# A finer cut around the end of each filter unit, and a denser schedule of weight preparation, beside attention

## The chip, the cores and the metric

The kernel runs on 1 core of a Trainium2 chip. The metric is the device time of one execution in microseconds (us); less is better. Inputs and outputs are in float32.

## The reference

Two layers act on 2048 tokens of width 1024. The first has a pooling mixer beside attention (6 query heads, 2 key heads, 2304 keys: 256 of the context and 2048 of the tokens). The second has a long convolution (Hyena) beside a Fourier mixer. The change touches the stage that computes attention and, beside it, the filters of the second layer's convolution and its prepared weights. Cut to that:

```python
s = einsum('bqhgd,bkhd->bhgqk', q, k) * scale     # attention, layer 0
p = softmax(s, axis=-1)
yb = einsum('bhgqk,bkhd->bqhgd', p, v) * silu(b_gate)
...
h = (hdn @ w3).reshape(L, 2, 2, 768)              # filters, layer 1
h = h * decay
h = h / (sum(abs(h), axis=(0, 2)) + EPS)          # one sum for each filter
kf = fft(concat(h[:, :, 0], 0, reversed h[:, :, 1]))
```

## The kernel before, in words

The stages run one after the other: projections of layer 0 (to about 605 us), attention (to about 1776 us), the output projection of layer 0 with the first columns of layer 1, then layer 1. In the attention stage the order of every engine's instructions is the order in which the Python code records them; nothing is moved there by a planner. Names used below: PE multiplies, DVE, ACT and POOL are vector engines, SP issues the DMAs. Each engine takes its instructions in the order given.

**Attention.** There are 96 blocks of 128 queries; two blocks, one even and one odd, make a pair of 256 queries of one head, so there are 48 pairs, here numbered 0 to 47. A string in `BLOCK` (L44) lists what a block records, token by token: `S0` to `S4` are the scores of the *next* block against 512 keys (three matmuls each, L315 to L317, then a maximum on DVE, L1323), `M` the maximum over all, `E0` to `E4` the exponentials on ACT (L1334), `Z` their sum, `T0` to `T4` the transposition of this block's exponentials on PE (L1345) with a split into a high and a low part (ACT L309, DVE L312), `V0` to `V4` the products with the values (L1357 to L1361). `D` and `N` finish the pair before: ACT puts the reciprocal sums on a diagonal, PE multiplies that by ones (`prb`, L1374), and DVE multiplies the result with the gate and the output (`rb`, L1376 and L1377). After each even block SP stores `rb` and loads the queries of two pairs later.

**Filters.** `F` takes one step of the generator `filters` (L1119); `f` does so only in every `MORE`-th pair. There are 12 units (6 channel groups by 2 orders). A unit has 8 groups of two steps: one with the product `hacc` (L1194), which DVE multiplies with the decay into `ht` (L1195) and reduces into `rd` (L1198), and one with the product `fa` (L1231), which ACT copies into `fX` (L1232). Both products share one PSUM buffer, `psF`, so each of them waits until the one ahead has been read. In the last group come two steps more: DVE sums `rd` over the 8 groups into `rs` (L1204), PE multiplies `rs` by ones (`smacc`, L1207), and DVE makes the scales and `sd` from it (`scaled`, from L1213); the last `fa` (L1229) needs `sd`. That makes 18 steps for a unit. Then the unit's transform of length 16 is queued for POOL (L155, L158, L193), in pieces that `some` (L1131) hands out at nearly every later step, up to 4.4 us of planned POOL time each; a transform takes 13 such pieces. The spectrum `fX` is stored four pieces later.

**Weight preparation.** `p` takes one step of the generator `weights` (L1399). First come 23 pieces of the second layer's input weights: SP loads `wraw`, one step on ACT copies it into the high part of `wodd` (L1409), one step on POOL subtracts to get the low part (L1411), two steps on SP stores it and, in the same step, loads the next piece. `wraw` has two buffers and `wodd` one. Then come 32 pieces of the two output weights, with one more stage: POOL multiplies `wraw` by a gate (L1431) one step after the load, and two steps after that ACT copies. A piece of the first kind takes 4 steps, one of the second 6. At the end come two small products `fnp` on PE (L1446). All in all that is 92 + 192 + 12 steps. With six `p` in a pair they would take over 49 pairs; when the filters are through, `fill` (L1469) runs what is left of `weights` at once, then frees the memory, and from then on the blocks follow the third and fourth string and each `F` takes two steps of `wout` (L1386), which loads the 8 output weights `w` of layer 0 and the first two pieces of `y`.

**After attention** the output projection starts with `oacc` (L315 to L317); it needs `w` and the split `y` (ACT L1628, DVE L1629).

Of the kernel before, what the change touches and what calls it, by code (L numbers as in the profile page):

```python
# [20 lines left out]
P = 128  # L21
# [20 lines left out]
PAIRS = [(n, N2 - n) for n in range(1, 8)] + [(0, 8)]  # L42

BLOCK = [  # L44
# [204 lines left out]
def tile_net(ctx, tc, i, k, out, keep=None):  # L249
# [230 lines left out]
            split_to(hf[:, :w], hi[:, :w], lo[:, :w], v, lo_eng[m % 2])  # L480
            yield 1.3, 0.0

    LASTE, LASTR, GATE2, FOLD1, HALF, SUM0, SUM1, ADDF, FEW, LASTW, IN_C, FFT_US, FFT_LATE, FILTER_X, HL, DR, DE, EW0, EW1, SPLIT, SUMMED, QSEL, CV0, CV1, CV2, CV3, COL, NW0, NW1, FIRST_Z, MORE, X0_SQ, X0_STEP, TRAIL, C_EARLY, A_TURN, A_SLOW, A_AHEAD, A_W, A_PACE, LAG0, FOLD, WAIT, AHEAD, LAG, APART, LOW, W_LOAD, W_HIGH, W_LOW, ADDED, SLOW = 0, 0.5, 5, 6, 1.5, 0.2, 1.5, 3, 9, 3.5, 25, 4.4, 4, 2, 3, 4, 4, 8.0, 2.5, 15, 0.5, 1, 14, 12, 8, 15, 5, 24, 0, 20.0, 8, [7, 7, 11, 11], (0, 0, 0, 0, 2, 2, 2, 2), 11, 1, 2.5, 0.25, 3.5, 4, 1.05, 7, 2, 6.0, 2.5, 5, 5, 2, 6, 6, 4, 8, 1.02

    xr = i["x"][0].rearrange("(p b) d -> p b d", b=N2)
    outr = out[0].rearrange("(p b) d -> p b d", b=N2)
# [632 lines left out]
    def filters(st, psum, tag, after):  # L1119
# [59 lines left out]
        for u in range(2 * NCH):  # L1179
            j, o = u // 2, u % 2  # L1180
            w3, skr = got.pop(u)
            rd = sp.tile([P, 8, P], F32, tag="rd", name="rd")
            X = sp.tile([P, 2, N2, P], F32, tag="X", name="fX", bufs=FILTER_X)
            for grp, (n, m) in enumerate(PAIRS):
                last = grp == 7
                if (u, grp) != (2 * NCH - 1, 7):
                    fetch(u + grp // 7, (grp + 1) % 8)
                dec, hd = got.pop((u, grp))
                ht = sp.tile([P, 2, 2, P], F32, tag="ht", name="ht", bufs=2)
                acc = psum.tile([P, 2, 2, P], F32, tag=tag, name="hacc")  # L1190
                for q in range(2):
                    for x in range(2):
                        w = w3[:, x, ::-1] if q else w3[:, x]
                        pe.matmul(acc[:, q], hd[:, q, :], w, start=x == 0, stop=x == 1)  # L1194
                after(1, lambda: v.tensor_mul(ht, acc, dec.unsqueeze(2).to_broadcast([P, 2, 2, P])))  # L1195
                yield
                some()
                v.tensor_reduce(out=rd[:, grp, :], in_=ht.rearrange("p a d b -> p b (a d)"), axis=AX.X, op=ALU.add,  # L1198
                                apply_absolute_value=True)
                if u + 1 < 2 * NCH and grp in (3, 6):  # L1200
                    (fetch_w3 if grp == 3 else split_w3)(u + 1)
                if last:
                    rs = sp.tile([P, P], F32, tag="rs", name="rs")
                    v.tensor_reduce(out=rs, in_=rd.rearrange("p a b -> p b a"), axis=AX.X, op=ALU.add)  # L1204
                    yield
                    sm = psum.tile([P, 512], F32, tag=tag, name="smacc")
                    pe.matmul(sm[:, 0:1], rs, ones[:, 0:1], start=True, stop=True)  # L1207
                    pe.matmul(sm[0:1, P : 2 * P], ones[:, 0:1], rs, start=True, stop=True)
                    sd = sp.tile([P, 2, 2, P], F32, tag="ht", name="sd", bufs=2)

                    def scaled():
                        idx = o * NCH + j
                        v.tensor_scalar(out=sc_n[:, idx : idx + 1], in0=sm[:, 0:1], scalar1=EPS, scalar2=None, op0=ALU.add)  # L1213
                        rw = sp.tile([1, P], F32, tag="rw", name="rw")
                        v.scalar_tensor_tensor(out=rw, in0=sm[0:1, P : 2 * P], scalar=EPS, in1=skr, op0=ALU.add, op1=ALU.mult)
                        v.reciprocal(sc_n[:, idx : idx + 1], sc_n[:, idx : idx + 1])
                        v.tensor_add(ht[0:1, 0, 0, :], ht[0:1, 0, 0, :], rw)
                        v.memset(ht[0:1, 0, 1, :], 0.0)
                        v.tensor_add(sd[:, 0], ht[:, :, 0], ht[:, :, 1])
                        v.tensor_sub(sd[:, 1], ht[:, :, 0], ht[:, :, 1])  # L1220


                    after(2, scaled)
                    yield
                fa = psum.tile([P, 2, 2, P], F32, tag=tag, name="fa")
                for r in range(2):
                    for q, b in enumerate((n, m)):
                        if last:
                            pe.matmul(fa[:, r, q], dft[:, b, r, :], sd[:, r, q], start=True, stop=True)  # L1229
                        else:  # L1230
                            pe.matmul(fa[:, r], dft[:, b, r, :], ht[:, q], start=q == 0, stop=q == 1)  # L1231
                after(3, lambda: s.copy(X[:, :, n : m + 1 : m - n, :], fa))  # L1232
                yield
                if last:
                    T = sp.tile([P, 2, N2, P], F32, tag="T", name="fT")
                    ops += [(0.04 + 2.05 * us, fn) for fn, us in fft16(g, X, T, False, g, True)]
                    ops.append((0.0, (specd[j][o], X)))
                some()
# [20 lines left out]
    with ExitStack() as st:  # L1259
# [108 lines left out]
        def finish(key):  # L1368
            h, tb = key
            gr = groups.pop(key)  # L1370
            tl = slice(tb * 256, (tb + 1) * 256)
            pr = psT.tile([P, 2, P], F32, tag="pt", name="prb")
            for b, dg in enumerate(dgs.pop(key)):
                pe.matmul(pr[:, b, :], ones, dg, start=True, stop=True)  # L1374
            rb = sp.tile([P, 256], F32, tag="rb", name="rb")
            v.tensor_mul(rb, pr.rearrange("p a b -> p (a b)"), gr["sg"])  # L1376
            v.tensor_mul(rb, gr["o"], rb)  # L1377
            stores.append((y0d[2 + h][:, tl], rb))

        def store():  # L1380
            while stores:
# [17 lines left out]
        def weights():  # L1399
# [22 lines left out]
            for n, (src, dst) in enumerate(((i["ev_w_out"][0], wevd), (i["od_w_out"][0], wod))):  # L1422
                for half in range(2):
                    hl = slice(half * 512, half * 512 + 512)
                    gb = wp.tile([P, 512], F32, tag="gate", name="wgb")
                    sy.dma_start(gb, gated[n].rearrange("(o a) b -> o (a b)", o=1)[:, hl].to_broadcast([P, 512]))
                    for kk in range(KD):
                        raw = raws()
                        sy.dma_start(raw, src[kk * P : (kk + 1) * P, hl])
                        yield  # L1430
                        g.tensor_mul(raw, raw, gb)  # L1431
                        yield
                        yield
                        yield from parts(raw, dst[kk][:, :, hl])
            fw = raws().rearrange("p (a e) -> p a e", a=2)
# [49 lines left out]
        with tc.manual_schedule(engines=EVERY):  # L1485
# [53 lines left out]
            values(before, 4)  # L1539
            diagonals(before)  # L1540
            finish(before)
            store()
            while queue:
                fill()
# [875 lines left out]
```

## Time and profile before

| | us |
|---|---|
| median of 3 runs | 3170.09 |
| lowest and highest | 3164.2, 3178.07 |
| the profiled execution's own time | 3180.38 |
| its span, first to last instruction | 3178.6 |
| PE busy, of the span | 2935.4 |
| DVE, ACT, POOL busy | 2146.7, 1325.2, 1131.8 |
| granted TensorE clock, mean | 0.968 |

PE is busy 92% of the span, the others 36% to 68%. A busy PE is not a PE at its peak, since matmuls are pipelined and their ends are modelled. In the rows of a timeline the first number is the start, the second the duration, and brackets hold the idle time ahead and what ended it. In rows of waits the numbers are the total in us, the count and the longest.

### The profile page before, as it was taken

What the parts mean: (1) busy time and instruction counts of PE and PEld (TensorE: products, weight loads), DVE (VectorE), ACT (ScalarE), POOL (GpSimd) and SP (SyncE); (2) the same over time, 40 slices, a digit from 0 to 9 for tenths busy, and PEclk for the clock granted to TensorE, in tenths of its full rate; (3) what the DMA queues carried; (4) which work ended last, traced back from release to release, by engine and by line L of the source; (5) the groups of instructions that cost most, each with busy time, mean ns of one, the idle gap of its engine ahead of it and who ended that gap; (6) DMA issues with size and microseconds to landing.
All of it is one profiled execution on the core that took longest, in us unless ns stands there. A gap on an engine that the chain in (4) does not pass through costs nothing. (4 is left out here: it accounts for less than half of the span.)

```text
span 3178.6 us, 46875 instructions
## 1 busy us (share of the span) xinstructions
PE 2935.4 (92%) x16969; PEld 2519.8 (79%) x16969; DVE 2146.7 (68%) x3981; ACT 1325.2 (42%) x3047; POOL 1131.8 (36%) x1091
## 2 busy tenths in 40 slices
PE   7899999799999999999986999999989999988799
PEld 4898888688888888888875778777878787874577
DVE  4676436477777777777764343377789797978556
ACT  4444545365555555555554232322323222232223
POOL 3122222127768787777772344001010000101110
PEclk9999999899999999999998999999999999999899
DMA  6466335533433334333325676688898989876875
GB/s 219 149 203 206 119 134 165 177 98 123 128 124 120 110 121 131 112 107 113 114 77 193 213 265 244 241 267 275 267 310 272 292 280 307 274 251 184 217 206 175
DMA packets 346707, 602.74 MB, mean 190 GB/s; under 512 B 41894, under 2 KB 216168, under 8 KB 336490
## 3 DMA queue, kind: packets, MB, share of 16 engines
q1 hardware_dynamic: 321322, 516.63, 47.8%
q0 software_dynamic: 25152, 83.10, 11.2%
q8 instruction: 134, 2.20, 0.3%
q14 instruction: 99, 0.81, 0.1%
HBM read 376.80 MB, written 187.18 MB: 177 GB/s over the span
## 5 line engine op out<-in xcount | busy, mean ns | idle before, releaser
L312 DVE TENSOR_TENSOR pl<-pt,ph 128x512 fp32r<-128x512 f32 (+1 forms) x480 | 300.1, 634 | 160.0 <-ACT ph L309 153.6
L155 DVE TENSOR_TENSOR gB<-gB 128x256 f32<-128x256 f32 (+3 forms) x442 | 351.6, 845 | 51.5 <-ACT gB L1927 47.7
L1334 ACT ACTIVATE pb<-S,mx 128x512 f32<-128x512 f32 (+1 forms) x480 | 310.7, 658 | 177.5 <-DVE mx L1326 143.3
L315 PE MATMUL dacc<-dh,dw 128*128 128x512 f32 x768 | 311.4, 405 | 46.5 <-DMA dh<-h1T 45.4
L309 ACT CAST ph<-pt 128x512 fp32r<-128x512 f32 (+1 forms) x480 | 256.2, 557 | 216.9 <-PE pt L1345 215.0
L316 PE MATMUL dacc<-dh,dw 128*128 128x512 f32 x768 | 304.4, 396 | 0.0
L317 PE MATMUL dacc<-dh,dw 128*128 128x512 f32 x768 | 304.1, 396 | 0.0
L1323 DVE TENSOR_REDUCE mx<-S 128x1 f32<-128x512 f32 (+1 forms) x480 | 279.5, 629 | 8.9 <-PE S L317 8.7
L1345 PE MATMUL pt<-ident,pb 128*128 128x128 f32 x1728 | 251.3, 275 | 21.4 <-ACT pb L1334 20.0
L312 POOL TENSOR_TENSOR wl<-raw,wh 128x256 fp32r<-128x256 f32 x160 | 134.8, 873 | 373.3 <-ACT wh L309 347.6
L1357 PE MATMUL o<-ph,vh 128*128 128x256 f32 x864 | 237.9, 306 | 0.2
L1345 PEld LDWEIGHTS pt<-ident,pb 128*128 128x128 f32 x1728 | 200.2, 141 | 41.3 <-ACT pb L1334 29.8
L315 PE MATMUL S<-kh,qh 128*128 128x512 f32 (+1 forms) x480 | 200.0, 417 | 30.1 <-DVE pl L312 15.4
L1358 PE MATMUL o<-ph,vl 128*128 128x256 f32 x864 | 220.4, 286 | 1.8 <-DMA vl<-vl 1.8
L155 POOL TENSOR_TENSOR fX<-fT 128x256 f32<-128x256 f32 (+2 forms) x168 | 219.2, 1328 | 2.6
L315 PEld LDWEIGHTS dacc<-dh,dw 128*128 128x128 f32 x768 | 147.7, 192 | 85.0 <-DMA dh<-h1T 43.4
L155 POOL TENSOR_TENSOR fT<-fX 128x1024 f32<-128x1024 f32 (+2 forms) x120 | 190.8, 1622 | 58.4 <-ACT fX L1232 56.6
L315 PE MATMUL acc<-wh,hh 128*128 128x256 f32 x672 | 198.8, 296 | 5.4 <-DVE hh L311 2.6
L317 PE MATMUL acc<-wh,hl 128*128 128x256 f32 x672 | 194.0, 289 | 1.0 <-DVE hl L312 0.9
L316 PE MATMUL acc<-wl,hh 128*128 128x256 f32 x672 | 194.1, 289 | 0.9 <-POOL wl L312 0.8
L316 PE MATMUL S<-kl,qh 128*128 128x512 f32 (+1 forms) x480 | 182.2, 379 | 1.3 <-DMA kl<-kT1l 1.3
L317 PE MATMUL S<-kh,ql 128*128 128x512 f32 (+1 forms) x480 | 181.9, 379 | 0.0
(475 smaller groups left out, 7397.5 us busy)
## 6 DMA issues: line engine op xcount, KB each, us to landing
dh<-h1T SPq DMA_DIRECT2D x172, 512.0 KB
spec<-fX SPq DMA_DIRECT2D x12, 2048.0 KB
dw<-wi SPq DMA_DIRECT2D x48, 512.0 KB
gK<-spec SPq DMA_DIRECT2D x48, 512.0 KB
raw<-in_ev_w_in_dram SPq DMA_DIRECT2D x160, 128.0 KB
u<-dev SPq DMA_DIRECT2D x70, 256.0 KB
cu<-u POOLq DMA_DIRECT2D x17, 1024.0 KB, 8.3
wmb<-in_w_mod_dram SPq DMA_DIRECT2D x16, 1024.0 KB
```

Source lines behind the costliest of these rows:

```text
L155: put(out, lambda: v.tensor_tensor(out=out, in0=in0, in1=in1, op=op))
L309: s.copy(hi, src)
L312: lo_eng.tensor_sub(lo, src, hi.bitcast(F32))
L315: pe.matmul(acc, ah, bh, start=first, stop=False)
L316: pe.matmul(acc, ah, bl, start=False, stop=False)
L317: pe.matmul(acc, al, bh, start=False, stop=last)
L1323: v.tensor_reduce(out=B["mx"][:, c : c + 1], in_=S[:, :n], axis=AX.X, op=ALU.max)
L1334: s.activation(B["pb"][:, c * 512 : c * 512 + n], B["S"][c][:, :n], AF.Exp, bias=B["mx"][:, 5:6], accum_out=B["sm"][:, c : c + 1])
L1345: pe.transpose(pt[:, t, :], B["pb"][:, (4 * c + t) * P : (4 * c + t + 1) * P], ident)
L1357: pe.matmul(gr["o"], vh[:, a, :], ph[:, t, :], start=a == 0, stop=False)
L1358: pe.matmul(gr["o"], vl[:, a, :], ph[:, t, :], start=False, stop=False)
```

## The change

It has five edits, all in the attention stage.

1. `MORE` goes from 8 to 2: the `f` step is taken in every second pair instead of every eighth.
2. A unit of filters takes 20 steps instead of 18. The sum over the groups is made in two parts: groups 0 to 3 go into `rd[:, 4]` in group 5, and the five columns 4 to 8 into `rs` at the end, two tokens after their step begins. A step stands between that and the product `smacc`, and another between `scaled` and the last `fa`; both hand out a piece of the transform.
3. The even block's string gets one `p` more, so there are seven in a pair.
4. In the 32 pieces with a gate, ACT's copy stands one step behind POOL's product instead of two: a piece takes 5 steps, and the whole of `weights` 92 + 160 + 12.
5. The two products of `rb` are recorded two tokens after `N`, and flushed at the end of the stage.

```diff
-    "T0 p S0 S1 F S2 S3 S4 M T1 f p F D V3 V4 E1 N E3 T2 E0 T3 p E4 E2 F T4 Z",
+    "T0 p S0 S1 F S2 S3 S4 M T1 f p F D V3 V4 E1 N E3 T2 E0 T3 p E4 E2 F T4 p Z",
...
-            rd = sp.tile([P, 8, P], F32, tag="rd", name="rd")
+            rd = sp.tile([P, 9, P], F32, tag="rd", name="rd")
...
-                v.tensor_reduce(out=rd[:, grp, :], in_=ht.rearrange("p a d b -> p b (a d)"), axis=AX.X, op=ALU.add,
+                v.tensor_reduce(out=rd[:, grp + grp // 4, :], in_=ht.rearrange("p a d b -> p b (a d)"), axis=AX.X, op=ALU.add,
                                 apply_absolute_value=True)
...
+                if grp == 5:
+                    v.tensor_reduce(out=rd[:, 4, :], in_=rd[:, :4].rearrange("p a b -> p b a"), axis=AX.X, op=ALU.add)
                 if last:
-                    rs = sp.tile([P, P], F32, tag="rs", name="rs")
-                    v.tensor_reduce(out=rs, in_=rd.rearrange("p a b -> p b a"), axis=AX.X, op=ALU.add)
+                    rs = rd[:, 0, :]
+                    after(2, lambda: v.tensor_reduce(out=rs, in_=rd[:, 4:].rearrange("p a b -> p b a"), axis=AX.X, op=ALU.add))
+                    yield
+                    some()
                     yield
...
                     after(2, scaled)
+                    yield
+                    some()
                     yield
...
-            v.tensor_mul(rb, pr.rearrange("p a b -> p (a b)"), gr["sg"])
-            v.tensor_mul(rb, gr["o"], rb)
-            stores.append((y0d[2 + h][:, tl], rb))
+
+            def gated():
+                v.tensor_mul(rb, pr.rearrange("p a b -> p (a b)"), gr["sg"])
+                v.tensor_mul(rb, gr["o"], rb)
+                stores.append((y0d[2 + h][:, tl], rb))
+
+            after(2, gated)
...
                         g.tensor_mul(raw, raw, gb)
-                        yield
                         yield
                         yield from parts(raw, dst[kk][:, :, hl])
...
             finish(before)
+            flush()
             store()
```

Edit 1 is the one number `MORE` in the long line of numbers at L483.

Three places show what moves. The first is PE in the even block of pair 3 or so, at the `f` token. Before, the product `hacc` is followed by the values:

```order
L1345 MATMUL pt<-ident,pb 128x128 x4
L1194 MATMUL hacc<-w3s,hd 128x256 x4
L1357 MATMUL o<-ph,vh_6890 128x256
L1358 MATMUL o<-ph,vl_6891 128x256
L1357 MATMUL o<-ph,vh_6890 128x256
```

Now `fa` of the same group stands right behind it:

```order
L1351 MATMUL pt<-ident,pb 128x128 x4
L1194 MATMUL hacc<-w3s,hd 128x256 x4
L1237 MATMUL fa<-ht,fdft 128x256 x4
L1363 MATMUL o<-ph,vh_6890 128x256
L1364 MATMUL o<-ph,vl_6891 128x256
```

The `f` of a pair has moved a product of the filters to where another one follows at once. It does so in every second pair now.

The second place is POOL late in a transform, beside the pieces with a gate (`wraw<-wraw,wgb` is the product with the gate, `wodd<-wraw,wodd` the subtraction that follows ACT's copy). Before:

```order
L158 TENSOR_SCALAR fX<-fX 128x4x128
L1431 TENSOR_TENSOR wraw<-wraw,wgb 128x512
L158 TENSOR_SCALAR fT<-fT 128x4x128
L155 TENSOR_TENSOR fX<-fX,fT 128x4x128
L155 TENSOR_TENSOR fX<-fT,fX 128x4x128
L155 TENSOR_TENSOR fX<-fT 128x2x2x128 x2
L1411 TENSOR_TENSOR wodd<-wraw,wodd 128x512
L1431 TENSOR_TENSOR wraw<-wraw,wgb 128x512
```

Now, in a transform of the same phase:

```order
L155 TENSOR_TENSOR fT<-fX,fT 128x4x128
L155 TENSOR_TENSOR fT<-fT,fX 128x4x128
L155 TENSOR_TENSOR fX<-fT 128x4x128
L155 TENSOR_TENSOR fT<-fT 128x4x128
L1441 TENSOR_TENSOR wraw<-wraw,wgb 128x512
L1421 TENSOR_TENSOR wodd<-wraw,wodd 128x512
L155 TENSOR_TENSOR fX<-fT 128x2x128 x4
```

Five instructions of the transform stood between the product and the subtraction; now none does, and more of them stand ahead of the product.

The third place is SP at the end of the stage (`w0_n` are the output weights of layer 0, `cxt` the residual rows, `y0_n<-y0_85` the pieces of `y`, `y0_85<-rb` the stores of finished pairs). Before:

```order
L261 DMA w0_6_20296<-we6_215 128x2048
L261 DMA w0_7_20298<-we7_216 128x2048
L1246 DMA y0_20395<-y0_85 128x8x128
L1246 DMA y0_20397<-y0_85 128x8x128
L261 DMA y0_85<-rb_20411 128x256
L1618 DMA cxt_20579<-in_x_dram 128x2048
L1618 DMA cxt_20581<-in_x_dram 128x2048
```

Now:

```order
L1628 DMA cxt_20579<-in_x_dram 128x2048
L1628 DMA cxt_20581<-in_x_dram 128x2048
L261 DMA y0_85<-rb_20527 128x256
L261 DMA w0_6_20531<-we6_215 128x2048
L261 DMA w0_7_20533<-we7_216 128x2048
L1252 DMA y0_20538<-y0_85 128x8x128
L1252 DMA y0_20540<-y0_85 128x8x128
```

The last two weights and the first pieces of `y` have moved behind the residual rows and behind the store of the last pair.

More of the change, by code (lines that the diff above doesn't have):

```diff
@@ L481, in modulated_steps @@
             yield 1.3, 0.0
-    LASTE, LASTR, GATE2, FOLD1, HALF, SUM0, SUM1, ADDF, FEW, LASTW, IN_C, FFT_US, FFT_LATE, FILTER_X, HL, DR, DE, EW0, EW1, SPLIT, SUMMED, QSEL, CV0, CV1, CV2, CV3, COL, NW0, NW1, FIRST_Z, MORE, X0_SQ, X0_STEP, TRAIL, C_EARLY, A_TURN, A_SLOW, A_AHEAD, A_W, A_PACE, LAG0, FOLD, WAIT, AHEAD, LAG, APART, LOW, W_LOAD, W_HIGH, W_LOW, ADDED, SLOW = 0, 0.5, 5, 6, 1.5, 0.2, 1.5, 3, 9, 3.5, 25, 4.4, 4, 2, 3, 4, 4, 8.0, 2.5, 15, 0.5, 1, 14, 12, 8, 15, 5, 24, 0, 20.0, 8, [7, 7, 11, 11], (0, 0, 0, 0, 2, 2, 2, 2), 11, 1, 2.5, 0.25, 3.5, 4, 1.05, 7, 2, 6.0, 2.5, 5, 5, 2, 6, 6, 4, 8, 1.02
+    LASTE, LASTR, GATE2, FOLD1, HALF, SUM0, SUM1, ADDF, FEW, LASTW, IN_C, FFT_US, FFT_LATE, FILTER_X, HL, DR, DE, EW0, EW1, SPLIT, SUMMED, QSEL, CV0, CV1, CV2, CV3, COL, NW0, NW1, FIRST_Z, MORE, X0_SQ, X0_STEP, TRAIL, C_EARLY, A_TURN, A_SLOW, A_AHEAD, A_W, A_PACE, LAG0, FOLD, WAIT, AHEAD, LAG, APART, LOW, W_LOAD, W_HIGH, W_LOW, ADDED, SLOW = 0, 0.5, 5, 6, 1.5, 0.2, 1.5, 3, 9, 3.5, 25, 4.4, 4, 2, 3, 4, 4, 8.0, 2.5, 15, 0.5, 1, 14, 12, 8, 15, 5, 24, 0, 20.0, 2, [7, 7, 11, 11], (0, 0, 0, 0, 2, 2, 2, 2), 11, 1, 2.5, 0.25, 3.5, 4, 1.05, 7, 2, 6.0, 2.5, 5, 5, 2, 6, 6, 4, 8, 1.02
     xr = i["x"][0].rearrange("(p b) d -> p b d", b=N2)
```

## The prediction

> **What bounds the kernel now.** I read the page first, then busy time by stretches of the attention stage, then the waits of that stage, then single rows.
>
> The page gives each engine's share, and the span in 40 slices:
>
> ```profile
> PE 2935.4 (92%) x16969; PEld 2519.8 (79%) x16969; DVE 2146.7 (68%) x3981; ACT 1325.2 (42%) x3047; POOL 1131.8 (36%) x1091
> POOL 3122222127768787777772344001010000101110
> ```
>
> PE sets the time. POOL, at 36% overall, is 70% to 80% busy in slices 10 to 20, which is the stage that the change edits. By stretches (columns: from:to, length, then each engine's busy time, granted clock, DMA share, GB/s) that is a generic pair, a pair with a unit's end, a pair with its `f`, the last pairs one by one, and 60 us over one whole transform:
>
> ```profile
> 731.60:754.50 22.90, 22.62 (x151) 20.59 (x150) 16.96 (x33) 13.93 (x36) 22.37 (x25) 1.00 0.33 97
> 754.50:779.10 24.60, 22.59 (x159) 20.22 (x159) 19.77 (x35) 13.82 (x36) 9.18 (x8) 1.00 0.48 168
> 800.90:826.90 26.00, 24.19 (x162) 22.03 (x161) 18.25 (x34) 14.12 (x36) 25.30 (x25) 1.00 0.34 102
> 1634.20:1655.90 21.70, 18.54 (x126) 16.00 (x125) 13.16 (x29) 12.45 (x33) 21.23 (x22) 1.00 0.21 61
> 1655.90:1682.40 26.50, 21.08 (x126) 18.26 (x125) 13.43 (x29) 12.34 (x33) 25.13 (x24) 0.87 0.22 77
> 1682.40:1730.50 48.10, 25.31 (x135) 20.82 (x134) 13.76 (x30) 15.21 (x38) 6.34 (x5) 0.75 0.48 174
> 1730.50:1749.20 18.70, 17.62 (x127) 15.80 (x126) 13.19 (x29) 12.06 (x32) 0.00 (x0) 1.00 0.73 283
> 783.80:843.80 60.00, 57.91 (x388) 53.01 (x387) 43.77 (x84) 34.92 (x92) 58.90 (x50) 1.00 0.34 102
> ```
>
> A generic pair is full on PE (22.62 of 22.90). Two kinds of place are not: pairs with a unit's end (2 us idle), and the three stretches from 1634, where the filters' products have run out and weight preparation has not. There a pair needs no more than the 18.70 of the row at 1730.50, and takes up to 48.10. In the 60 us over a transform POOL is busy for 58.90: it has no slack. The waits of the stage (engine, line, what released it: total, times, longest):
>
> ```profile
> PE S L315 <- DVE pl L312: 11.9, 6, 4.6
> ...
> PE fa L1229 <- DVE sd L1219: 7.8, 4, 2.8
> ACT wodd L1409 <- POOL wraw L1431: 7.3, 2, 4.9
> PE smacc L1207 <- DVE rs L1204: 6.3, 6, 1.9
> ```
>
> The second and fourth row are PE's waits at a unit's end; ACT waits for POOL's gate product only twice so far.
>
> **The change, part by part.**
>
> *Drain gone: -36.* Weight preparation has 92 + 192 + 12 steps at six a pair, 49 pairs, and so is unfinished at pair 45. The three stretches from 1634.20 take 21.70 + 26.50 + 48.10 = 96.3 us; three pairs at 18.70 are 56.1; 40.2 are lost. Now 264 steps at seven a pair end in pair 38, inside attention. The two products `fnp` do not vanish; warm they cost PE about 2.0 each, as the eight matmuls `fa` of the same shape here (cold, after 16.81 idle, they took 3.75):
>
> ```profile
> 814.05 1.99 PE L1231 MATMUL fa<-ht,fdft 128*128 128x256 f32 x8 [1.58 <-DVE ht L1195]
> ...
> 1707.12 3.75 PE L1446 MATMUL fnp<-wraw 128*128 128x256 f32 x8 [16.81 <-DMA wraw<-cst_dftd_dram]
> ```
>
> 40.2 - 4 = 36. What comes next there is the filters themselves: 240 steps at 5.5 a pair are 43.6 pairs, where 216 at 5.13 were 42.1, so they end 1.5 pairs later and the last transform in pair 46, one pair ahead of the end. That is nothing lost, but no margin either.
>
> *Unit ends: -20 (10 to 42).* The steps now set between `rs`, `smacc`, `scaled` and the last `fa` aim at 7.8 + 6.3 us in the waits and at 5.2 of the 11.9 of `S` (the other 6.7 fall behind 1634): 19.3 by the waits, and by the stretches 12 x (24.60 - 22.90) = 20.4. I take 20. Half is the low end, since `scaled` still stands on DVE ahead of the split `pl` that PE's next products need; the upper end takes twice the 1.7 of the stretches at each of 12 ends. The added partial sum lies on DVE at 68%: nothing.
>
> *`f` next to `F`: +15.* An `f` moves a product next to the following one, both through one PSUM buffer: when `fa` lands behind `hacc` it waits for DVE's `ht` (the 1.58 above), the other way round for ACT's copy:
>
> ```profile
> 1389.66 0.74 PE L1194 MATMUL hacc<-w3s,hd 128*128 128x256 f32 x4 [0.68 <-ACT fX L1232]
> ```
>
> With `MORE` 8 there were two of each; with 2 there are eight of each: 6 x 1.58 + 6 x 0.68 = 13.6, and a little for the slower start after it, 15. Below 0 it cannot go: one buffer allows no overlap.
>
> *ACT's copies wait for POOL in transforms: +36 (5 to 66).* In the 60 us above POOL's own transform work is 58.90 less three subtractions of 1.30, so 55. Before, 13 pieces at 5.1 a pair stretched over 13 / 5.1 x 22.9 = 58 us, and POOL had 55 + 2.55 weight pieces of 2.57 (1.30 and 1.27) = 61.6 to do: 3 late at the end. Now 13 pieces at 5.5 a pair take 54 us, and seven steps a pair at five a piece make 1.4 weight pieces a pair: 55 + 2.36 x 1.4 x 2.57 = 63.5, that is 9.4 late. And ACT's copy stands one step behind POOL's product, 3.3 us instead of 7.6. How little room there was is seen in two pairs of rows, product and copy:
>
> ```profile
> 1426.40 1.30 POOL L1431 TENSOR_TENSOR wraw<-wraw,wgb 128x512 f32<-128x512 f32 x1
> 1427.80 0.64 ACT L1409 CAST wodd<-wraw 128x512 fp32r<-128x512 f32 x1
> ...
> 1153.14 1.27 POOL L1431 TENSOR_TENSOR wraw<-wraw,wgb 128x512 f32<-128x512 f32 x1
> 1156.53 0.63 ACT L1409 CAST wodd<-wraw 128x512 fp32r<-128x512 f32 x1
> ```
>
> The copy began 0.1 and 2.1 us after the product's end. Where that was used up, ACT stood, and behind the copy in its queue are the next `E` and the split `ph` that PE's products wait for:
>
> ```profile
> 1662.32 1.26 POOL L1431 TENSOR_TENSOR wraw<-wraw,wgb 128x512 f32<-128x512 f32 x1
> 1663.62 0.62 ACT L1409 CAST wodd<-wraw 128x512 fp32r<-128x512 f32 x1 [4.88 <-POOL wraw L1431]
> 1665.50 0.79 PE L315 MATMUL S<-kh,qh 128*128 128x512 f32 x1 [4.57 <-DVE pl L312]
> ```
>
> Of ACT's 4.88, 4.57 reached PE. Not every wait passes on so; a copy just ahead of an exponential that waits for the maximum anyway has this cover:
>
> ```profile
> 921.28 0.69 ACT L1334 ACTIVATE pb<-S,mx 128x512 f32<-128x512 f32 x1 [3.63 <-DVE mx L1326]
> ```
>
> So one transform costs between nothing and 9.4 - 2.1 = 7.3. With cover 9.4 - 3.63 = 5.8; a copy due one weight piece before the end of the transform 3.2; I take 3.5 for nine transforms (those of units 0 to 8; by then preparation is over): 31. In the pair of that 4.57 the granted clock was 0.87, of 21.08 busy us 2.7 lost; I put two such into the sum, 5: together 36. The low end is 5, hidden but for about what ACT waits today; the high end 9 x 7.3 = 66.
>
> The Trainium skill, in "TensorE: Matmul & The Clock Gate", section "What's actually happening", has a rule that bears on this price: after an idle window of about 3.4 us the array runs at half rate, until about 3.4 us of sustained work have passed. An estimate by that page is 1.7 us for each such gap instead of 2.7, and the sum would be 2 lower.
>
> *End of the stage: +18 (16 to 20).* With `F` done so late, `wout`'s last two weights and the first two pieces of `y` stand on SP behind `cxt` and behind the last store, which waits for DVE's last `rb`. In before they were long under way:
>
> ```profile
> 1775.08 0.83 SPq L1618 DMA_DIRECT2D cxt<-in_x_dram  x2
> 1753.92 1.05 ACT L1628 CAST y<-y 128x1024 fp32r<-128x1024 f32 x1 [2.40 <-DMA y<-y]
> 1776.05 0.47 PE L315 MATMUL oacc<-w,y 128*128 128x512 f32 x1 [0.56 <-issue]
> ```
>
> Two stretches show what the DMA engines can move (the last number is GB/s):
>
> ```profile
> 1724.00:1735.00 11.00, 9.75 (x69) 8.79 (x68) 6.83 (x17) 7.01 (x20) 0.00 (x0) 1.00 1.02 410
> 1775.00:1785.00 10.00, 9.44 (x45) 7.73 (x44) 1.54 (x3) 0.00 (x0) 1.83 (x3) 1.00 0.94 319
> ```
>
> Ahead of `oacc` there now go two rows `cxt` and two `w` of 1.05 MB and one `y` of 0.52: 4.7 MB at 410 or 319 GB/s, the fullest rows, 11.5 to 14.8 us. With the cast of 1.05, landing, the clock's 2.7, less 0.56, that is 16 to 20. What follows is full on PE, so it passes to the end.
>
> *`rb` two tokens later: 0.* In the blocks with filters only ACT's `E` lie between, so DVE's order stays. The extra `p` itself is ACT and POOL work, priced above.
>
> Sum: -36 - 20 + 15 + 36 + 18 = **+13**. The profiled execution's own time is 3180.38; it would become 3193. The median of the runs lies 10.3 under that, so on the median 3170.09 + 13 = **3183**.
>
> **The rivals.**
>
> *POOL becomes the bound inside transforms; slower.* The waits pass on as at 1665.50: +66 instead of +36, which gives 3183 + 30 = 3213. For it: 4.57 of 4.88, and the margin of 0.1. Against it: the covers of 3.63. It decides once those waits cost PE over 39 us, 4.3 a transform.
>
> *POOL's lateness is hidden; faster.* +5 instead of +36, and unit ends give 30 instead of 20: 3183 - 41 = 3142. For it: ACT is busy only 14 of 23 us a pair, and waited for POOL twice in the whole stage. Against it: 9.4 us late where margins were 2. It falls below 3154 at under 0.8 a transform with the other terms as summed.
>
> *The change does not do what it says.* Preparation ends in time, but the same work is only spread: the waits of ACT and POOL take the tail's 36 back, about 1 us in each of 38 pairs, and what unit ends give, 20, goes to `f` and to the start of `oacc`. That is within 5 us of 3170. For it: all the pieces are still there and only closer together; against it, the 16.81 in which PE did nothing at all.
>
> **How the numbers follow.** About 0.5%, 16 us, is what a measurement of this kernel tells from no change: faster is under 3154, slower over 3186. My case has 0.5, with a range of its own of 3165 to 3201; of that 0.30 is the same and 0.20 slower. The slower rival has 0.22, the faster one 0.18, the third 0.10 (0.08 same, 0.02 faster). That makes 0.20 faster, 0.38 same, 0.42 slower. The range from 3142 to 3218 reaches to both rivals' values and leaves about a fifth outside.
>
> **What would show it.** Right: stretches after pair 45 of 18 to 19 us with no 16.81 gap; `ACT wodd <- POOL wraw` up from 7.3 to 40 or more; eight waits of `fa` near 1.58; PE idle 14 us or more ahead of the first `oacc`. Wrong: POOL's product stays a microsecond ahead of the copy through a whole transform; `oacc` starts at once; or pairs of a unit's end still take 24.6.

## The result, and the profile after

| | before | changed |
|---|---|---|
| median of the runs side by side, us | 3169.0 (3164.2 to 3178.07) | 3202.71 (3200.69 to 3206.37) |
| ratio | | 1.0104, 95% interval 1.008 to 1.0129 |
| the profiled execution's own time | 3180.38 | 3206.37 |
| from the first `M` of the stage to the `M` with which the last pair begins | 616.6 to 1749.2: 1132.6 | 620.2 to 1760.1: 1139.9 |
| from that `M` to the first `oacc` | 26.9 | 42.2 |
| from the first `oacc` to the end | 1402.6 | 1402.2 |

Below, "the last `M`" is the one with which the last pair begins, the 95th of the 96. The changed kernel is 33.7 us slower by the medians and 26.0 by the two profiled executions. Of these 26.0, 3.6 lie ahead of the first `M`. In the other profiles of this study, ten of them of kernels with the same start as the changed one, the first `M` lies anywhere from 610.4 to 618.6, so these 3.6 are put down to the execution, which is argued and not shown. What is left is +7.3 inside attention and +15.3 at its end.

The page of the changed kernel:

```profile
PE 2945.7 (92%) x16969; PEld 2520.3 (79%) x16969; DVE 2155.2 (67%) x3993; ACT 1323.5 (41%) x3047; POOL 1130.1 (35%) x1091
POOL 3122123116777776677666344000010100101110
```

PE, ACT and POOL execute as many instructions as before, DVE 12 more (the partial sums). PE is busy 10.3 us longer with the same matmuls, and POOL does its work in one slice more, at a lower share. Now single pairs (busy times, the share of full speed that PE's clock was granted, DMA share, GB/s): pairs 6 and 28, each with a unit's end, and pairs 44 to 46, after the filters' last product.

```profile
764.00:793.70 29.70, 23.83 (x151) 20.86 (x150) 20.04 (x36) 14.23 (x37) 12.05 (x10) 0.89 0.54 185
1310.10:1339.50 29.40, 23.61 (x146) 20.95 (x146) 20.11 (x42) 13.64 (x36) 10.76 (x10) 0.88 0.51 173
1702.80:1721.70 18.90, 17.67 (x123) 15.65 (x123) 13.17 (x29) 11.71 (x32) 18.68 (x11) 1.00 0.09 29
1721.70:1740.60 18.90, 18.05 (x126) 16.03 (x126) 13.17 (x29) 11.71 (x32) 18.26 (x22) 1.00 0.10 29
1740.60:1760.10 19.50, 17.39 (x119) 15.08 (x118) 13.79 (x30) 12.29 (x33) 13.84 (x15) 1.00 0.26 107
```

The drain is gone: the last pairs take 18.9 to 19.5, where three stretches of before took 96.3 together. But pairs inside attention now take up to 31.9 (pair 16), and the two shown here have 6 us of PE's idle time and a granted clock of 0.89 and 0.88. The waits from the first `M` to the last:

```profile
PE fa L1237 <- DVE ht L1195: 13.1, 8, 1.9
PE hacc L1194 <- ACT fX L1238: 10.6, 11, 3.0
...
PE smacc L1211 <- DVE rd L1206: 2.9, 2, 2.6
...
PE fa L1235 <- DVE sd L1223: 0.5, 1, 0.5
```

```profile
ACT wodd L1419 <- POOL wraw L1441: 46.2, 11, 9.3
ACT wodd L1419 <- DMA wraw<-in_od_w_in_dram: 27.1, 6, 6.2
```

The waits at a unit's end have shrunk from 14.8 us to 3.9. In exchange the waits at `f` grew from 3.2 to 13.1 and from 2.4 to 10.6, and ACT's copies wait 46.2 for POOL (before: 7.3 up to 1690 and 15.9 up to the last `M`) and 27.1 for the load of the first pieces (2.7 before). The longest of the first kind, in pair 28, on POOL, ACT and PE:

```profile
1313.02 1.26 POOL L155 TENSOR_TENSOR fX<-fT 128x512 f32<-128x512 f32 x1
1314.23 1.26 POOL L1441 TENSOR_TENSOR wraw<-wraw,wgb 128x512 f32<-128x512 f32 x1
1315.53 0.62 ACT L1419 CAST wodd<-wraw 128x512 fp32r<-128x512 f32 x1 [9.29 <-POOL wraw L1441]
1316.88 1.33 PE L1351 MATMUL pt<-ident,pb 128*128 128x128 f32 x5 [4.00 <-ACT pb L1340]
```

POOL works without a gap through instructions of the transform that stand ahead of the product. ACT stands for 9.29, and 4.00 of that is left as idle time of PE, since its transpositions need the exponentials queued behind the copy. One of the second kind, in pair 6, on POOL, SP and ACT:

```profile
765.86 1.29 POOL L1421 TENSOR_TENSOR wodd<-wraw,wodd 128x512 fp32r<-128x512 f32 x1
767.18 0.32 SPq L261 DMA_DIRECT2D wi<-wodd  x1
767.55 1.29 SPq L497 DMA_DIRECT2D wraw<-in_od_w_in_dram  x2
773.02 0.62 ACT L1419 CAST wodd<-wraw 128x512 fp32r<-128x512 f32 x1 [5.68 <-DMA wraw<-in_od_w_in_dram]
```

Here it is the subtraction that is late. SP's store waits for it, the load of a later piece stands behind the store, and a copy one step behind the load waits for its landing. PE's next scores start at 774.90, after 4.85 us of idle time.

The end of the stage, on SP, ACT and PE:

```profile
1781.93 0.81 SPq L1628 DMA_DIRECT2D cxt<-in_x_dram  x2
1783.29 0.33 SPq L261 DMA_DIRECT2D y<-rb  x1
1783.66 2.50 SPq L261 DMA_DIRECT2D w<-we  x2
1786.21 8.68 SPq L1252 DMA_DIRECT2D y<-y  x2
1801.22 1.04 ACT L1638 CAST y<-y 128x1024 fp32r<-128x1024 f32 x1 [20.46 <-POOL iw L1794]
1802.32 0.80 PE L315 MATMUL oacc<-w,y 128*128 128x512 f32 x1 [19.97 <-ACT y L1638]
```

PE stands for 19.97 us where it stood for 0.56, which is 19.4 more, and yet the gap is only 15.3 longer. The rest was won just ahead of it. In before, ACT's cast of `y` stood inside the last pair and waited 2.40 us for its load (the row at 1753.92), and PE stood there for 1.57, 1.18 and 1.15 us; from the last pair's first `M` to its second took 13.3 us. Now the cast comes later, and it takes 8.8. (POOL's `iw` in the brackets is what came last by the profile; the cast needs `y`, which SP began to issue at 1786.21.)

### The profile page after: what moved, and what is told of

It is laid out like the page before. It is cut to its first block, busy times and chain, and to the rows that moved or that the text cites. A ratio compares the mean times of both kernels' runs of the same rounds, so it can differ in the third digit from the quotient of the medians.

```text
span 3204.6 us, 46836 instructions
## 1 busy us (share of the span) xinstructions
PE 2945.7 (92%) x16969; PEld 2520.3 (79%) x16969; DVE 2155.2 (67%) x3993; ACT 1323.5 (41%) x3047; POOL 1130.1 (35%) x1091
## 3 DMA queue, kind: packets, MB, share of 16 engines
q1 hardware_dynamic: 321322, 516.63, 47.4%
## 5 line engine op out<-in xcount | busy, mean ns | idle before, releaser
L315 PE MATMUL S<-kh,qh 128*128 128x512 f32 (+1 forms) x480 | 198.9, 414 | 21.5 <-DVE pl L312 13.5
```

What stands on the lines that cost most here:

```text
L315: pe.matmul(acc, ah, bh, start=first, stop=False)
```

## The experiments

Each kernel is the changed one or the one before with the edit shown. Ratios are to the kernel before on the same chip, with the 95% interval; "the stretch" is from the first `M` to the last of the profiled execution, 1139.9 us in the changed kernel, "the gap" from the last `M` to the first `oacc`, 42.2 us.

**The weights earlier.**

```diff
-            for _ in range(len(ready) + 1):
+            for _ in range(2 * len(ready) + 1):
```

> The changed kernel, but once the filters are through each F takes three steps of wout instead of two, so that all eight weights and the first two pieces of y are under way on SP before the last block is. Theory (SP's order at the end of the stage is what PE stands for ahead of oacc): PE's idle time ahead of the first oacc falls from 19.97 us to under 3, and the time from 3202.7 to about 3184 (3180 to 3190). Rival (the DMA engines are full there whatever the order, and POOL's chain for iw takes its share): 10 us or more of the idle time stay and the time stays over 3193.

Measured: 3182.52 us, ratio 1.006 (1.0048 to 1.0072). The stretch is 1137.8, the gap 32.5. On PE and on SP:

```profile
1764.24 10.06 SPq L1252 DMA_DIRECT2D y<-y  x2
1781.75 0.79 PE L315 MATMUL oacc<-w,y 128*128 128x512 f32 x1 [10.18 <-ACT y L1638]
```

```profile
1765.00:1770.00 5.00, 5.00 (x44) 5.00 (x44) 1.98 (x4) 1.55 (x4) 2.43 (x3) 1.00 0.99 391
1770.00:1775.00 5.00, 1.57 (x14) 1.38 (x12) 0.85 (x2) 0.00 (x0) 0.00 (x0) 1.00 1.04 425
```

Half of PE's idle time went, and the two cases share the outcome: 10.18 us stay, as the rival had it, while the time is where the theory had it (3182.52; by the ratio and the 3169.0 of before it would be 3188). `y` was issued 11 us earlier after the last `M` (14.9 instead of 26.1) and still landed late, at a DMA share of 0.99 and 1.04. The order on SP is about half of the cause; what remains is put down to the 8.4 MB of weights that can only start when the filters are through, which the next run tries.

**`y` ahead of the weights.** The edit above, and in `wout`:

```diff
             wop = pool(woside, "w_o", 1, side="right")
-            for kk in range(KD):
-                w = wop.tile([P, 2, D], F32R, name=f"w0_{kk}")
-                mv(w, wevd[kk])
-                wo[kk] = w[:, 0], w[:, 1]
-                yield
+            ws = [wop.tile([P, 2, D], F32R, name=f"w0_{kk}") for kk in range(KD)]
             yps.append(pool(woside, "c_ya", 2, side="right"))
             for t in range(2):
                 ys[t] = load_y(yps[0], t)
             yield
+            for kk, w in enumerate(ws):
+                mv(w, wevd[kk])
+                wo[kk] = w[:, 0], w[:, 1]
+                yield
```

> The changed kernel with three steps of wout per F, as in the run with the earlier weights, and with the two pieces of y loaded ahead of the eight weights instead of behind them. In that run 10.18 us of idle time stayed ahead of oacc, with the DMA engines at 390 to 425 GB/s throughout. Theory (the filters end too late for 8.4 MB of weights, and y stood last in that queue; the first oacc needs only y and w0, its last products come 5 us later): the idle time ahead of the first oacc falls to under 3 us, and the time another 5 to 9 below that run, a ratio to before of 1.003 to 1.0045. Rival (the volume is what counts, whichever comes last): PE stands as long for the weights, ratio 1.005 to 1.007.

Measured: 3190.01 us, ratio 1.0069 (1.0043 to 1.0095).

```profile
1777.07 0.47 PE L315 MATMUL oacc<-w,y 128*128 128x512 f32 x1 [0.56 <-issue]
1781.76 0.50 PE L315 MATMUL oacc<-w,y 128*128 128x512 f32 x1 [1.04 <-DMA w<-we]
1784.70 0.80 PE L315 MATMUL oacc<-w,y 128*128 128x512 f32 x1 [1.97 <-DMA w<-we]
1787.84 0.79 PE L315 MATMUL oacc<-w,y 128*128 128x512 f32 x1 [1.49 <-DMA w<-we]
```

`oacc` begins at once (the gap is 23.9), and then stands for the weights. The 97th matmul of `oacc` starts 30.6 us after the first, against 21.9 in before: 8.7 later, as long as what the earlier start gained (32.5 - 23.9 = 8.6). The ratio is no lower than in the run before. The rival was right: the volume counts, not what stands last in the queue.

**The copy two steps behind again** (edit 4 undone).

```diff
                         g.tensor_mul(raw, raw, gb)
                         yield
+                        yield
                         yield from parts(raw, dst[kk][:, :, hl])
```

> The changed kernel with edit 4 undone: ACT's copy stands two steps behind POOL's product again, 296 steps at seven a pair, so preparation ends in pair 42 or 43, still inside attention. Theory (copies that wait for a late POOL cost PE some 25 to 35 us): ACT's wait for the gate product falls from 46.2 us to under 15 and the time by 15 to 30, to 3173 to 3188. Rival (the loss inside attention is f's and the extra p's): the wait falls, but the time stays within 6 of 3202.7.

Measured: 3176.7 us, ratio 1.005 (1.0036 to 1.0064). The stretch is 1126.8, 13.1 shorter. The two kinds of ACT's waits:

```profile
ACT wodd L1419 <- DMA wraw<-in_od_w_in_dram: 26.2, 6, 6.1
ACT wodd L1419 <- POOL wraw L1441: 11.9, 4, 6.0
```

The wait for POOL's product fell from 46.2 to 11.9, as the theory had it, and the time with it; the second kind stayed. The stretch gained 13.1 for 34 us of ACT's waits.

**A fifth step for the first pieces.**

```diff
                     load_columns(raw[...], n // KD, n % KD, half)
                 yield
+                yield
                 yield from parts(raw, wid[n // KD][n % KD])
```

> The changed kernel with one step more between the load of a piece of the input weights and ACT's copy of it: five steps a piece for the first 23 pieces, 287 in all. Theory (the seventh p set the copy too close behind a load that SP can issue only after the store, which waits for POOL's subtraction): ACT's waits for that load fall from 27.1 to under 8 us, pairs 6 and 10, which took 29.7 and 27.8, take under 26.5 each, and the time falls by 6 to 14, a ratio of 1.006 to 1.0085. Rival (these pairs are long because of the unit's end in them): they stay within 1.5 us, ratio 1.0095 or more.

Measured: 3186.91 us, ratio 1.0056 (1.0036 to 1.0075), the stretch 1130.6. Pairs 6 and 10 took 22.1 and 23.4 and no wait for the load of these pieces is left. But:

```profile
ACT wodd L1419 <- POOL wraw L1442: 57.5, 15, 10.1
```

The other wait rose from 46.2 to 57.5. The later pieces now fall on other places of the transforms, and part of what was won (12.0 us in the two pairs) was lost there: the stretch is only 9.3 shorter. The theory has the two pairs and the load's wait right, the rival is refuted, and the ratio comes out just under the theory's range.

**Smaller pieces of the transform.** In the line of numbers `FFT_US` goes from 4.4 to 3.4; copies stay one step behind.

> The changed kernel with smaller pieces of the transform: 3.4 us of planned POOL time a step instead of 4.4, so 16 pieces instead of 13. Theory (POOL is late because 55 us of transform and 8 of weights are squeezed into 13 / 5.5 pairs, 54 us; 16 pieces take 67 us for 55 + 2.9 x 1.4 x 2.57 = 65): ACT's waits for the gate product fall from 46.2 to under 12 us and those for the load of the first pieces from 27.1 to under 10, and the stretch from the first M to the last falls from 1139.9 by 15 to 25. The filters then end about half a pair later and oacc starts 5 to 20 later still, so that the time gains little: a ratio of 1.004 to 1.010. Rival (a copy one step behind the product waits however POOL is loaded): the waits stay over 35 and the stretch within 6.

Measured: 3175.18 us, ratio 1.0031 (1.0015 to 1.0046). The stretch is 1109.5, 30.4 shorter, the gap 47.4.

```profile
ACT wodd L1419 <- DMA wraw<-in_od_w_in_dram: 9.2, 4, 2.7
ACT wodd L1419 <- POOL wraw L1441: 5.4, 4, 3.1
```

With the copy still one step behind the product both kinds of waits are nearly gone. So a copy one step behind does not wait of itself: it waits where POOL is late in the transform. The distance sets how much of that lateness shows, since two steps hid most of the first kind. Of the edits tried on the changed kernel this one number has the largest effect inside attention: more than the 15 to 25 us that were expected, with a ratio a little under the expected 1.004. The stretch of the changed kernel and of this one (length, then busy times of PE, PEld, DVE, ACT and POOL, granted clock, DMA share, GB/s):

```profile
620.20:1760.10 1139.90, 1059.26 (x6990) 950.95 (x6991) 823.94 (x1624) 637.93 (x1665) 770.87 (x639) 0.98 0.36 115
613.60:1723.10 1109.50, 1044.23 (x6997) 942.51 (x6998) 822.77 (x1622) 638.18 (x1664) 771.89 (x639) 0.99 0.37 118
```

Only half of the 30.4 us is idle time of PE. The other 15.0 is busy time: PE does as many matmuls in less of it, at a higher granted clock. As foretold, the filters end later for it, and PE stands 24.8 us ahead of `oacc`.

**`f` apart from `F`.**

```diff
-    "T0 p S0 S1 F S2 S3 S4 M T1 f p F D V3 V4 E1 N E3 T2 E0 T3 p E4 E2 F T4 p Z",
+    "T0 p S0 S1 F S2 S3 S4 M T1 p F D V3 V4 E1 N E3 f T2 E0 T3 p E4 E2 F T4 p Z",
```

> The changed kernel with the f of the even string moved from two tokens ahead of F to behind the second E3, six tokens from the F before it; the count of steps stays. Theory (f costs because two products of the filters in a row share one PSUM buffer): the waits of 1.58 for ht and of 0.68 for fX go, 13 us in sum (8 to 18), to 3190. Rival (the products meet with something else wherever f stands, or their waits are covered later in the pair): within 5 of 3202.7.

Measured: 3181.22 us, ratio 1.0055 (1.004 to 1.007). The stretch is 1126.5, 13.4 shorter.

```profile
PE hacc L1194 <- ACT fX L1238: 19.3, 12, 3.6
PE fa L1237 <- DVE ht L1195: 1.6, 7, 0.2
```

The waits for `ht` went from 13.1 to 1.6. The waits for `fX` did not go, they rose to 19.3, the longest 3.6, not the 0.68. The sum of 13 came out with 11.5 from one of its two parts. Some of the rest is the clock. In the changed kernel the wait of 1.92 us for `ht` that ends at 679.90 in pair 2 is followed by a slow clock:

```profile
680.00:682.00 2.00, 2.00 (x6) 1.60 (x7) 1.25 (x2) 0.00 (x0) 0.00 (x0) 0.59 0.44 125
```

With `f` apart the granted clock of that pair is 1.00 instead of 0.94, and it takes 24.8 us instead of 28.1.

**18 steps in a unit** (edit 2 undone, the other four kept; the diff is that part of the change, reversed).

> The changed kernel with edit 2 undone: 18 steps in a unit and one sum over all groups, so the filters also end earlier and SP loads the weights in time. Theory (the two added steps are worth some 20 us at 12 unit ends, and cost the late start of oacc): PE's waits for rs and sd come back to some 14 us, the stretch from the first M to the last gets 10 to 20 longer, PE's idle time ahead of oacc is under 2, in sum within 6 of the changed kernel, ratio 1.0085 to 1.0125. Rival (the added steps only move the waits elsewhere): the stretch stays within 5, and only the end gets shorter, ratio 1.004 to 1.0065.

Measured: 3195.1 us, ratio 1.0085 (1.0065 to 1.0104). The stretch is 1151.5, 11.6 longer; the gap 22.9, since the filters end in time.

```profile
PE smacc L1207 <- DVE rs L1204: 19.1, 9, 4.4
...
PE fa L1229 <- DVE sd L1219: 5.7, 3, 2.7
```

The waits at unit ends come back, 24.8 us of them, but the stretch is only 11.6 longer; where the difference stays hidden is not shown. And the two added steps cost 42.2 - 22.9 = 19.3 at the end. By these profiles edit 2 loses more at the end than it gains inside; the intervals of the two ratios overlap, so the medians do not show it. The theory holds in its ratio, the stretch and the start of `oacc`; the waits came back with more than its 14.

**`rb` at once** (edit 5 undone; the two products and the append stand behind `rb` again).

> The changed kernel with edit 5 undone: the two products of rb are recorded with N again. Theory (only ACT's exponentials lie between in the blocks with filters): nothing, the stretch from the first M to the last within 3 us, ratio 1.009 to 1.0115. Rival (the later products hold up a PSUM buffer that PE's next transposition needs, three waits of 1.7 in sum for rb): 4 or more faster; or, the other way, DVE waits for prb longer: 5 or more slower.

Measured: 3192.3 us, ratio 1.0078 (1.0057 to 1.0099). The stretch is 1137.5, 2.4 shorter, within the theory's 3; the ratio is a little under it, with an interval that reaches into it and overlaps the changed kernel's. An effect of edit 5 is not shown.

**The seventh `p` alone**, in the kernel before.

```diff
-    "T0 p S0 S1 F S2 S3 S4 M T1 f p F D V3 V4 E1 N E3 T2 E0 T3 p E4 E2 F T4 Z",
+    "T0 p S0 S1 F S2 S3 S4 M T1 f p F D V3 V4 E1 N E3 T2 E0 T3 p E4 E2 F T4 p Z",
```

> The kernel before with the seventh p alone (edit 3); nothing else changes, so a piece with a gate still has six steps and preparation ends near pair 42. Theory (the drain is worth 36, and pieces this far apart hardly wait): the gap of 16.81 is gone, ACT's wait for the gate product stays under 20, and the time is 3169 - 30 = 3139 (3130 to 3148). Rival (the tail's time comes back as waits in the pairs with transforms): 3160 to 3175.

Measured: 3156.26 us, ratio 0.9962 (0.9942 to 0.9981), 7.9 less by the medians. That misses both: neither 3139 nor 3160 and more. The profile has the drain gone (the last four pairs take 18.9, 18.9, 19.5 and 18.7, together 76.0, against 115.0 before) and a stretch of 1109.1, 23.5 shorter.

```profile
ACT wodd L1409 <- POOL wraw L1431: 15.6, 6, 5.5
ACT wodd L1409 <- DMA wraw<-in_od_w_in_dram: 14.0, 4, 5.0
```

Of 39 us in the last four pairs, 15.5 came back in the pairs before, where both kinds of waits grew (from 7.3 up to 1690, and from 2.7). The filters still end in pair 42, as in before, and PE stands only 0.56 us ahead of `oacc`. By the medians still less of it is left, on which more below.

**Four things mended together**: the weights earlier, `y` first, the copy two steps behind, `f` apart.

> The changed kernel with four things mended at once: three steps of wout per F, y ahead of the weights, the copy two steps behind the product again, and f apart from F. Theory (the three losses lie in different places and add): 15 + 13 + 13 us and the last gap of oacc off the changed kernel's time, a ratio to before of 0.994 to 0.998. Rival (the places share POOL's lateness, and what is mended in one turns up in the next pair): 1.0 to 1.004.

Measured: 3156.97 us, ratio 0.9968 (0.9955 to 0.998), the stretch 1114.1. The ratio is where the theory had it. The stretch lost 25.8 against 13.1 + 13.4 alone: these two add.

**And the fifth step for the first pieces on top.**

> The run with four things mended, and the fifth step for the first 23 pieces as well. Theory (that edit took 9 us off the stretch of the changed kernel by itself, in pairs that the four others don't touch): another 6 to 10 us less, a ratio to before of 0.993 to 0.9955. Rival (preparation, 319 steps, now ends so late that its last pieces and the products fnp meet the last transforms): 0.996 to 0.999.

Measured: 3133.89 us, ratio 0.9902 (0.988 to 0.9925), better than either case. The stretch is 1091.2, 22.9 shorter than with four, though that edit by itself had given 9.3.

```profile
ACT wodd L1419 <- POOL wraw L1442: 19.0, 9, 7.8
...
ACT wodd L1419 <- DMA wraw<-in_od_w_in_dram: 1.4, 1, 1.4
```

The wait for POOL's product rose by 5 with that edit (13.6 with four mended), where it had risen by 11 in the run with that edit alone: the shifted pieces seem to have met fewer late products here, which no run isolates. This kernel is 1.0% faster than the one before and 2% faster than the changed one.

**The kernel before once more**, unchanged, with a second profile.

> The kernel before once more, for a second profile, since the first one's time of 3180.38 was the highest of its runs but one by far. Theory (the stage of the change is the same in all executions, and the first execution was long elsewhere): the stretch from the first M to the last within 3 of 1132.6 and from there to oacc within 1 of 26.9, whatever the time. Rival (the drain or the change of the key head, both with waits for transfers, were long in that execution): the stretch is 8 or more shorter.

Measured: its own time is 3176.69, the stretch 1128.0, the gap 26.9. The 4.6 less lie between the two cases; most of them are pairs 10, 23 and 31, each about 1.5 shorter (pairs 10 and 31 with a granted clock of 1.00 instead of 0.93). The drain is the same, with a wait of 17.3 us ahead of `fnp` where there were 16.8.

## Why the prediction was right, and where it was off

Slower was the likeliest single direction, and the time lies in the range from 3142 to 3218. It is 20 over the 3183 and just past the likeliest case's own 3201. The signs and places of the terms held. The size held only because the range was wide: +13 was forecast, which by the prediction's own measure of 16 us is no change, and +33.7 was measured. In the profiles the terms miss by 9 us, mostly at the unit ends and the copies; 3.6 lie ahead of the stage and some 8 in the base that was taken.

All four signs of being right came: last pairs of 18.9 to 19.5, 46.2 us of ACT's waits for POOL, eight waits of `fa` with 13.1 in sum, and 19.97 us ahead of `oacc`. Of the signs of being wrong the first two did not come and the third is mixed: the twelve pairs with a unit's end take 20.0 to 29.7.

The terms, in us. The second, the third and the sixth measured one come from runs that take back or move one part of the change each, and the first from a run that makes one part alone; what the parts do together falls to the fourth, the remainder:

| term | predicted | measured | from |
|---|---|---|---|
| drain gone | -36 | -35 | last four pairs 115.0 to 76.0 with the seventh `p` alone, less 4 for `fnp` |
| unit ends | -20 (10 to 42) | -12 | stretch with 18 steps, 1151.5 against 1139.9 |
| `f` next to `F` | +15 | +13 | stretch with `f` apart, 1126.5 |
| ACT's copies | +36 (5 to 66) | +41 | remainder: what is left of the stretch's +7.3 |
| end of the stage | +18 (16 to 20) | +15 | gap, 42.2 against 26.9 |
| `rb` later | 0 | not shown (2) | stretch with `rb` at once, 1137.5 |
| sum | +13 | +22 | 26.0 less the 3.6 ahead of the stage |

**Drain.** Right, with its size and its place. What came next there was named as the filters, "nothing lost, but no margin either"; the margin was what the end of the stage then lacked.

**Unit ends.** The step that failed is the one that took PE's wait rows for time: most of the 7.8 + 6.3 us did go (3.9 are left with the smaller kinds), but the stretch gained only 12, and with 18 steps 20.9 us more of these waits cost only 11.6. Nor did the 5.2 of `S` show: that wait is 13.5 in sum now, 14.2 before. The low end of the range, argued from `scaled` still standing ahead of the split, was nearer.

**`f`.** Right as a mechanism for `ht`: eight waits, 13.1 us, gone when `f` stands apart. The smaller part, put on ACT's `fX`, is not shown, since those waits did not go. That such a wait also slows the clock was only "a little" in the term. Edit 1 itself was not taken back in any run; the run moves `f` instead.

**Copies.** Right in the mechanism, and the largest term: POOL is late inside a transform, and ACT stands at the copy with the exponentials behind it. The run with smaller pieces shows 30.4 of the 41: there 58.7 of ACT's 73.3 us of waits are gone. The remaining 10 are not shown. Three details were off. The working spoke of POOL's gate product alone; 27.1 of ACT's 73 us of waits come by another way, the late subtraction that holds SP's store and the load behind it, in the pieces that edit 4 doesn't touch. And the covers were right in kind (4.00 of 9.29 reached PE in pair 28), with a price a transform of 41 / 9 = 4.6 instead of 4. This lies just over the 4.3 from which the slower rival was to decide, but a remainder is not known to 2 us when two profiles of before differ by 4.6 in the stretch. What happened lies between the two cases, at two thirds of the rival's 66.

The third is the clock. It was in the sum as 2.7 us a gap, for two gaps. In steps of 2 us behind that gap of 4.00:

```profile
1314.00:1316.00 2.00, 0.00 (x0) 0.00 (x0) 0.00 (x0) 0.47 (x1) 2.00 (x3) 0.81 0.00 0
1316.00:1318.00 2.00, 1.12 (x5) 1.12 (x6) 0.00 (x0) 2.00 (x7) 1.94 (x2) 0.50 0.00 0
...
1320.00:1322.00 2.00, 2.00 (x10) 1.97 (x10) 1.26 (x5) 1.46 (x6) 0.00 (x0) 0.50 1.07 317
```

The 0.81 of the first row puts the fall at about 1315.2, and the clock is at one half up to 1322: 6.8 us, of which PE worked five, so some 2.6 are lost. By the trace's record of the granted clock, ten such slow spells begin between the first `M` and the last, seven of 3.4 us and three of 6.8; in the two profiles of before there are five and three of them up to pair 42. An estimate of what they cost, half of PE's busy time inside them, is 21.0 us for pairs 0 to 42 of the changed kernel, 13.3 and 7.2 in before, and 8.7 with smaller pieces. So the price of a gap was about right, 2.1 on average, but their number was not: the clock took 8 to 14 us more than before where the sum had 5. The Trainium skill ("TensorE: Matmul & The Clock Gate", section "What's actually happening") has the half rate and a warm-up of about 3.4 us; the half rate agrees with this trace, and so does the length in seven of the ten spells, while it is twice that in the other three.

**End of the stage.** The size came out right (15 for 18) with some luck, the cause only in part. PE's idle time ahead of `oacc` grew by 19.4; the 4.5 us that the last pair gained, since the cast of `y` no longer stands in it, were not in the sum. The prediction laid the wait to what SP issues late; the first of the two runs that moved those issues kept 10.18 us of idle time, the second moved the wait to the weights. What decides is when the filters end: with 18 steps, and so the filters' last product four pairs earlier (pair 39 instead of 43), the gap was 22.9, and with the seventh `p` alone, where they end in pair 42, PE stood for 0.56 us. So the later end of the filters, of which the prediction said "nothing lost", is what costs the start of `oacc`. The clock's 2.7 in this term was a miss: after 20 us of standing the first 96 matmuls of `oacc` did take 2.3 longer than before (24.2 against 21.9), but the 385th started 119.1 us after the first in both kernels. In all profiles without waits for weights it starts after 117.5 to 119.1 us where PE had not stood and after 117.9 to 120.4 where it had.

**The base.** The prediction took the change against one profiled execution and carried it over to the median. That step failed by some 8 us: 26.0 between the profiled executions, 33.7 between the medians. The profiled executions of before, 3180.38 and 3176.69, lie 11 and 9 over the medians of the runs beside them (3169.0 and 3168.19), and over the highest of these too; those of the changed kernel and of the run with the seventh `p` lie 4 over theirs, and those of the ten others from 6 under to 3 over. So the seventh `p` gains 17 to 20 by the profiles and 7.9 by the medians. The drain may cost less in executions without a profile; no run here shows that, and it stays open.

**The rivals.** The faster one fell with POOL's lateness, which was not hidden. The slower one has the mechanism, but not the whole of its 66. The third, that cost is only spread, fell too for the change as a whole, but the seventh `p` alone comes near it: 15.5 of its 39 came back as waits.

## What to carry to other kernels

Before more steps are packed beside a full engine, add up what the helper engines have to do in the same stretch: POOL had, by the prediction's estimate, 63.5 us of work for 54 us of pieces here, and one number that spread the pieces gave 30 of 1140 us back. The wait rows of the bounding engine are not its gain, either way: 20.9 us of waits at unit ends were worth 11.6, while with smaller pieces 15.4 us less of idle time came with a stretch 30.4 us shorter, since the slow clock behind the idle times went as well. Work that starts only when a generator ends should have its whole volume over the bandwidth set against the time left. Mended places can add up to less or to more than each alone (9.3 us alone, 22.9 with the others), so the last version must be run as a whole.

## What was not expected

PE's cold start after 20 us of standing cost 2.3 us by the 97th matmul and nothing clear of the spread of the profiles by the 385th, while 8.7 us of waits for weights at the same place were still there at the 385th (127.9 against 119.1). Why the one seems to be made up for and the other not was not tried. And gaps shorter than the idle window of about 3.4 us that the same section of the Trainium skill ("TensorE: Matmul & The Clock Gate") gives were enough for the clock to fall. The 1.92 us in pair 2, shown with the run that set `f` apart, are one; other idle times of the changed kernel, of 1.58 to 2.03 us, were not followed by a slow clock. Behind an idle time of 3.02 us, in pair 31, a row of the windows of the changed kernel reads

```profile
1394.00:1396.00 2.00, 2.00 (x12) 2.00 (x11) 1.90 (x4) 2.00 (x8) 2.00 (x4) 0.50 1.06 275
```
